# Two transformer blocks: the attentions' arithmetic moved from POOL to DVE and ACT, masks applied on DVE, and attention pieces written between projections

## The chip, the cores and the metric

The kernel runs on one core of one Trainium2 chip. The metric is the device time of one execution in microseconds (us), the median of three runs. The engines are TensorE (PE), VectorE (DVE), ScalarE (ACT), GpSimd (POOL) and SyncE (SP); each works through its own list of instructions in order, and semaphores tie the lists together.

## The reference

Input are 256 tokens of width 1024 and, in block 2, 16 meta tokens ahead of them.

```python
# block 1
h = x + mixer_block(rmsnorm(x), ...)      # sliding-window sink attention + retention, each gated, summed, @ w_out
h = h + squared_relu_mlp(rmsnorm(h), ...)
h = rmsnorm(h)
# block 2, on 16 meta tokens + 256 tokens
qa, ka, va, qb, kb, vb, g = split(rms_norm(h) @ w_in)
qa, ka, qb, kb = rope(qa), rope(ka), rope(qb), rope(kb)
# windowed: 16 query heads on 4 key heads; a key within +-128 positions, every meta key, and a sink logit
p = softmax(concat([where(mask, qa @ ka / 8, -1e30), s_meta, s_sink]))[:, :-1]
o_swa = p @ va
# differential: 8 heads, two softmaxes over all keys each
a = softmax(q1 @ k1 / 8) - lam * softmax(q2 @ k2 / 8)
o_diff = rms_norm(a @ vb) * 0.8
g_swa, g_diff = split(sigmoid(g + b_gate))
merged = g_swa * (o_swa @ w_branch_swa) + g_diff * (o_diff @ w_branch_diff)
h = h + rms_norm(merged @ w_out)
h = h + rms_norm((silu(gate) * up) @ w_ffn_out)
```

## The kernel before

**Weights.** All matrices are cut into 272 units of 128 x 1024 fp32 values (512 KB), in the order of use. SP loads a unit (`raw`), ACT casts it to the rounded part `hi` (L301, two halves of 128x512), DVE forms the rest `lo = raw - hi` (L303), and PE multiplies in three passes (hi·hi, hi·lo, lo·hi), so a unit costs 24 matmuls: of 256 columns where it gives 128 output features for the tokens (`mm_a`, L457), of 272 with the meta tokens, of 512 where the weights are the moving operand (`mm_b`, L469, and `mm_group`, L479). Activations are split alike (`split`: ACT casts, DVE subtracts, L329 and L330).

**Attention.** `rope_T` copies a projection from PSUM (`t`, ACT), has a copy with swapped halves made by DMAs that ACT issues (`sw`, L508 and L509), multiplies by cosines on DVE and by sines on POOL (L511), and adds on POOL (L514). `stack_q` and `stack_k` lay a head's hi and lo parts on the two halves of the partitions (`qe`, `qo`; `ks`, `kl`), with ACT, DVE and POOL. `scores` makes a head's 128 x n scores in PSUM, whose masked part is added by a matmul of an identity with a bf16 mask (`masksb`, L550): 24 of these in block 1, 32 in block 2. `sink_softmax` copies the sink logit beside them, takes the row minimum (the scores are negated), then exponential with its sum, reciprocal, and scaling (L561, L555, L565, L567, L568). `sink_attention`, here a piece, does four heads of one half of the queries; its transposed probabilities (`pt`) are split and multiplied with values (`o_ps`, L587), and the two halves of the result are added (`ol`, `of`).

**Block 1** (`block1`): values, gates, keys and queries of the retention (`vr`, `gr`, `kr`, `qr`), its heads (`ro`, `ry`, `yt_ps`), then the attention on four pieces with the table `rope_a`, which SP loads between two units.

**Block 2** (`block2`): values, `ka`, then for each of four query projections two pieces (eight in all); keys and queries of four pairs of differential heads (`at`, `atm`, `od`, `y`, `ot`), each pair followed by one projection for the first gate; then, in a phase `b3` of its own, the products `bs` of `os_t`, and per group the second gate and the product `bd` of `od_t`, which make `m2t`, the input of the output projection `op`.

**What sets the order.** The code is written in one sequence per engine, but a scheduler of the tile framework reorders each engine's list ahead of time by its own durations, within the dependences and within the numbers of buffers (`BUFS`; PSUM by `BANKS`: two banks each for `acc`, `tp` and `s`, one each for `pv` and `x`). Units are taken strictly in the order of the stream.

Of the kernel before, what the change touches and what calls it, by code (L numbers as in the profile page):

```python
# [37 lines left out]
VB1 = 2  # L38
# [33 lines left out]
def pack_weights(w_in, w_att_up, w_ret_up, w_out, w_ff1, w_ff2, w_in2, w_bs, w_bd, w_out2, w_fi, w_fo):  # L72
# [46 lines left out]
    in_a(w_in2, o_ka)
    for c in range(4):  # L120
        in_a(w_in2, o_qa + 256 * c)
        if c == VB1:
            in_a(w_in2, o_vb + 512)
            in_a(w_in2, o_vb + 768)
    for p in range(4):
        in_a(w_in2, o_kb + 256 * p)
        in_a(w_in2, o_qb + 256 * p)
        in_a(w_in2, o_g + 256 * p)
# [40 lines left out]
def make_consts():  # L169
# [54 lines left out]
class Body:  # L224
# [138 lines left out]
    def consts2(self):  # L363
        nc, cp, io = self.nc, self.cp, self.io
        cc = _CC
        mk = self.wp.tile([P, UC], F32, tag="raw", bufs=4, name="mk")[:, 0:3 * P]
        a, n = cc["masks"]
        nc.sync.dma_start(out=mk, in_=io["consts"][:, a:a + n])
        self.identb = cp.tile([P, P], BF16, name="identb")
        self.masks = cp.tile([P, 3 * P], BF16, name="masksb")  # L370
        nc.gpsimd.tensor_copy(self.identb, self.ident)
        nc.gpsimd.tensor_copy(self.masks, mk)
# [762 lines left out]
```

## Time and profile before

| | us |
|---|---|
| median of three runs (lowest, highest) | 917.32 (916.97, 918.11) |
| the profiled execution: time, span from first to last instruction | 916.5, 914.6 |
| PE busy | 887.4 (97%) |
| DVE, ACT, POOL busy | 628.5, 516.1, 176.7 |
| mean granted clock of TensorE | 0.996 of full speed |

Busy time is the sum of an engine's instructions; the issue of DMAs isn't in it. A time in the rows below is in us from the span's start, a mean in ns. A matmul's row gives when it began; the difference of two beginnings is its step.

### The profile page before, as it was taken

The page shows a single profiled execution, that of the slowest core. Times are in us where ns is not written, and L with a number is a line of the kernel's source. Part 1 is how long each engine was busy: PE and PEld are TensorE (multiplying, and loading weights), DVE is VectorE, ACT ScalarE, POOL GpSimd, SP SyncE. Part 2 cuts the span into 40 slices and gives each one's busy share as a digit, 9 for nine tenths or more (in the row PEclk, how much of TensorE's full clock was granted, in tenths as well). Part 3 has the DMA queues.
Part 4 walks back from the last instruction along what each step waited for, and adds up shares of the span by engine and source line. Part 5 has one row for each costly group of instructions (what it writes and reads, how often), then busy time and mean ns, then how long its engine had stood idle before and what let it go on. Part 6 is the DMA issues. An engine that isn't in the chain of part 4 may idle for free. (4 is left out here: it accounts for less than half of the span.)

```text
span 914.6 us, 16482 instructions
## 1 busy us (share of the span) xinstructions
PE 887.4 (97%) x6188; PEld 814.2 (89%) x6188; DVE 628.5 (69%) x1201; ACT 516.1 (56%) x1128; POOL 176.7 (19%) x181
## 2 busy tenths in 40 slices
PE   5999899999999999999999999999999999999997
PEld 3899889998899999987989878899999799999996
DVE  5466889667755555575689999988567675655654
ACT  4554357554655544565657778876455554544442
POOL 3013460101000011101273434551011100000000
PEclk9999999999999999999999999999999999999999
DMA  7675544468565665562664343433466656555641
GB/s 267 226 232 174 153 150 139 124 223 276 186 213 188 195 189 185 187 227 95 202 200 134 111 126 119 137 107 116 138 182 219 222 200 197 187 199 185 187 161 46
DMA packets 48126, 160.18 MB, mean 175 GB/s; under 512 B 6432, under 2 KB 8224, under 8 KB 48048
## 3 DMA queue, kind: packets, MB, share of 16 engines
q1 hardware_dynamic: 43376, 153.95, 52.1%
q10 hardware_dynamic: 4672, 5.20, 2.0%
q8 instruction: 48, 0.79, 0.3%
q14 instruction: 30, 0.25, 0.1%
HBM read 151.83 MB, written 2.10 MB: 168 GB/s over the span
## 5 line engine op out<-in xcount | busy, mean ns | idle before, releaser
L303 DVE TENSOR_TENSOR lo<-raw,hi 128x512 fp32r<-128x512 f32 x536 | 378.9, 749 | 188.5 <-ACT hi L301 185.3
L301 ACT CAST hi<-raw 128x512 fp32r<-128x512 f32 x532 | 301.8, 618 | 238.7 <-issue 81.8
L469 PE MATMUL op<-hi,hid 128*128 128x512 f32 x416 | 128.9, 390 | 0.0
L457 PE MATMUL fi_ps<-xf2t,hi 128*128 128x256 f32 x640 | 114.4, 281 | 0.0
L457 PEld LDWEIGHTS fi_ps<-xf2t,hi 128*128 128x128 f32 x640 | 99.1, 188 | 0.9
L457 PE MATMUL fi_ps<-xf2t,lo 128*128 128x256 f32 x320 | 90.1, 281 | 0.0
L469 PEld LDWEIGHTS op<-hi,hid 128*128 128x128 f32 x416 | 76.3, 188 | 14.6
L469 PE MATMUL op<-lo,hid 128*128 128x512 f32 x208 | 81.1, 392 | 0.0
L457 PE MATMUL f_ps<-xf1t,hi 128*128 128x256 f32 x448 | 80.5, 281 | 0.0
L457 PEld LDWEIGHTS f_ps<-xf1t,hi 128*128 128x128 f32 x448 | 69.9, 189 | 1.2
L457 PE MATMUL f_ps<-xf1t,lo 128*128 128x256 f32 x224 | 63.0, 281 | 0.0
L457 PEld LDWEIGHTS fi_ps<-xf2t,lo 128*128 128x128 f32 x320 | 60.6, 189 | 0.0
L457 PE MATMUL q_ps<-x2t,hi 128*128 128x256 f32 x256 | 50.3, 287 | 0.0
L457 PE MATMUL gate_ps<-x2t,hi 128*128 128x256 f32 x256 | 48.7, 285 | 0.0
L457 PE MATMUL gate_ps<-x1t,hi 128*128 128x256 f32 x256 | 48.5, 285 | 0.0
L418 POOL TENSOR_SCALAR e<-ss 128x1 f32<-128x1 f32 (+1 forms) x11 | 4.1, 372 | 221.1 <-ACT py L1031 192.2
L469 PEld LDWEIGHTS op<-lo,hid 128*128 128x128 f32 x208 | 39.0, 188 | 8.6
L798 POOL TENSOR_TENSOR sq<-relu 128x512 f32<-128x512 f32 x14 | 15.8, 1130 | 149.7 <-ACT relu L795 149.7
L457 PEld LDWEIGHTS f_ps<-xf1t,lo 128*128 128x128 f32 x224 | 42.4, 189 | 0.1
L457 PEld LDWEIGHTS q_ps<-x2t,hi 128*128 128x128 f32 x256 | 40.4, 189 | 0.8 <-issue 0.5
L457 PEld LDWEIGHTS gate_ps<-x2t,hi 128*128 128x128 f32 x256 | 39.9, 189 | 0.6 <-issue 0.5
L457 PEld LDWEIGHTS gate_ps<-x1t,hi 128*128 128x128 f32 x256 | 39.8, 189 | 0.2
(297 smaller groups left out, 2021.3 us busy)
## 6 DMA issues: line engine op xcount, KB each, us to landing
raw<-in_wstream_dram SPq DMA_DIRECT2D x272, 512.0 KB, 3.7
sw<-t ACTq DMA_DIRECT2D x40, 64.0 KB, 3.7
x<-in_x_dram SPq DMA_DIRECT2D x3, 512.0 KB, 6.5
sw<-t ACTq DMA_DIRECT2D x40, 34.0 KB, 2.2
sw<-t ACTq DMA_DIRECT2D x8, 128.0 KB, 3.5
g_pre<-in_gains_dram SPq DMA_DIRECT2D x2, 512.0 KB, 6.2
x<-hf SPq DMA_DIRECT2D x2, 512.0 KB, 2.7
x<-x SPq DMA_DIRECT2D x2, 512.0 KB, 6.2
```

The costliest lines, as they stand in the source:

```text
L301: nc.scalar.copy(hi[:, c:c + PIECE], raw[:, c:c + PIECE])
L303: nc.vector.tensor_sub(lo[:, c:c + PIECE], raw[:, c:c + PIECE], hi[:, c:c + PIECE].bitcast(F32))
L418: nc.gpsimd.tensor_scalar(out=e[:np_], in0=ss[:np_, 0:1], scalar1=1.0 / D, scalar2=EPS, op0=ALU.mult, op1=ALU.add)
L457: nc.tensor.matmul(out, wv[a][:, k, j * P:(j + 1) * P], XT[:, b, k, n0:n1], start=(i == 0), stop=(i == last))
L469: nc.tensor.matmul(out, XT[:, b, k0 + k, t0:t1], wv[a][:, k, c0:c0 + cn], start=(start and i == 0), stop=(stop and i == last))
L798: nc.gpsimd.tensor_tensor(out=q, in0=r, in1=r, op=ALU.mult)
```

## The change

The masks leave PE: a table of fp32 masks for the two halves of the queries stays in SBUF, and one DVE operation per head adds it, takes the minimum with the sink and writes the masked scores to `pn`. ACT scales by 1/den in place. Rope and the subtractions of `stack_q` are on DVE. `stack_k` splits once and places the parts by four DMAs. These DMAs, and in block 2 the swaps of `rope_T`, are issued by POOL. In block 2 the pieces, the differential heads, the projections, gates and products are written in turn, the phase `b3` is gone, and the stream of units follows. Buffers are dealt anew.

```diff
-        nc.gpsimd.tensor_tensor(out=sw, in0=sw, in1=S, op=ALU.mult)
+        nc.vector.tensor_mul(sw, sw, S)
-        nc.gpsimd.tensor_tensor(out=out, in0=t1, in1=sw, op=ALU.add)
+        nc.vector.tensor_add(out, t1, sw)
@@ stack_q (qo alike)
-        nc.gpsimd.tensor_tensor(out=qe[64:128], in0=qf[0:64], in1=qe[0:64].bitcast(F32), op=ALU.subtract)
+        nc.vector.tensor_sub(qe[64:128], qf[0:64], qe[0:64].bitcast(F32))
@@ stack_k
+        u = self.t([P, 2, n], "ku", F32R)
+        nc.scalar.copy(u[:, 0], kf)
+        nc.vector.tensor_sub(u[:, 1], kf, u[:, 0].bitcast(F32))
...
+            ks = self.t([P, 2, n], "ks", F32R)
+            for b in range(2):
+                nc.gpsimd.dma_start(out=ks[64 * b:64 * b + 64].bitcast(F32), in_=u[64 * e:64 * e + 64].bitcast(F32))
@@ scores
-        for i, (mi, c0) in enumerate(mask or ()):
-            nc.tensor.matmul(out[:, c0:c0 + P], self.identb, self.masks[:, mi * P:(mi + 1) * P],
-                             start=False, stop=(i == len(mask) - 1))
@@ sink_softmax
-        nc.vector.tensor_copy(s[:, n:n + 1], nsink)
-        nm = self.row_min(s)
+        nc.vector.tensor_tensor_reduce(out=p[:, :n], in0=s, in1=mask, scale=1.0, scalar=nsink, op0=ALU.add,
+                                       op1=ALU.min, accum_out=nm)
...
-        nc.vector.tensor_scalar(out=out, in0=p[:, :n], scalar1=rc, scalar2=None, op0=ALU.mult)
+        nc.scalar.activation(out=p[:, :n], in_=p[:, :n], func=AF.Copy, scale=rc)
@@ sink_attention
-        nc.scalar.copy(ol, o[64:128])
...
+            nc.scalar.copy(of[r], o[64:128, e:4:2])
+            nc.vector.tensor_add(of[r], o[0:64, e:4:2], of[r])
@@ block2
+        band(0, 0)
+        for i, b in v_T(4, "vb_ps"):
+            nc.scalar.copy(vall[i][:, 512:1024], b.rearrange("p m d -> p (m d)"))
+        band(0, 1)
+        q[2] = queries()
+        band(1, 0)
+        first_gate(0)
+        band(1, 1)
+        q[3] = queries()
+        band(2, 0)
+        first_gate(1)
+        band(2, 1)
+        kb = keys()
+        band(3, 0)
+        qb = queries()
+        first_gate(2)
+        band(3, 1)
+        first_gate(3)
...
+            self.diff_attention(qb, kb[0:2], vb, OD, 0, 2 * pr)
+            if pr < 3:
+                nk, nq = keys(), queries()
+            else:
+                first_product(3)
+                second_gate(2)
+            self.diff_attention(qb, kb[2:4], vb, OD, 1, 2 * pr + 1)
+            if pr < 3:
+                kb, qb = nk, nq
+                first_product(pr)
+                if pr < 2:
+                    second_gate(pr)
+            else:
+                second_gate(3)
```

On PE, within a piece of windowed attention of block 2, the scores `s` stand in the list of before like this (`vb_ps` is a projection).

```order
L547 MATMUL s<-ks,qe 128x272
L548 MATMUL s<-kl,qe 128x272
L550 LDWEIGHTS identb
L550 MATMUL s<-masksb,identb 128x128
L457 MATMUL vb_ps<-x2t,hi_5868 128x272
L457 MATMUL vb_ps<-x2t,lo_5869 128x272
L547 MATMUL s<-ks,qo 128x272
L548 MATMUL s<-kl,qo 128x272
L550 LDWEIGHTS identb
L550 MATMUL s<-masksb,identb 128x128
```

The masks' loads of the identity and matmuls are gone from every score of the change; here is such a place (`gate_ps` is a projection, `o_ps` a product with the values, `vT_ps` transposes of other values).

```order
L551 MATMUL s<-ks,qe 128x272
L552 MATMUL s<-ks,qe 128x272
L462 MATMUL gate_ps<-x2t,hi_5796 128x256
L961 MATMUL vT_ps<-ident,vt 128x128 x4
L551 MATMUL s<-ks,qo 128x272
L552 MATMUL s<-ks,qo 128x272
L462 MATMUL gate_ps<-x2t,hi_5796 128x256
L462 MATMUL gate_ps<-x2t,lo_5797 128x256
L590 MATMUL o_ps<-pt,va 128x512
```

A score is now its two products, and among the scores stand a gate's projection and the transposes of the values, in another order of the program. At the last piece of windowed attention PE's list of before has projections (`q_ps`) between scores and products `o_ps`:

```order
L547 MATMUL s<-ks,qe 128x272
L548 MATMUL s<-kl,qe 128x272
L457 MATMUL q_ps<-x2t,hi_7186 128x256
L457 MATMUL q_ps<-x2t,lo_7187 128x256
L457 MATMUL q_ps<-x2t,hi_7186 128x256 x2
L587 MATMUL o_ps<-pt,va 128x512
L457 MATMUL q_ps<-x2t,lo_7187 128x256
L457 MATMUL q_ps<-x2t,hi_7186 128x256 x2
L457 MATMUL q_ps<-x2t,lo_7187 128x256
L457 MATMUL q_ps<-x2t,hi_7186 128x256 x2
L457 MATMUL q_ps<-x2t,lo_7187 128x256
L457 MATMUL q_ps<-x2t,hi_7186 128x256 x2
```

In the change the last piece and the first differential head come together, and of projections only the first matmuls of `bs_ps` are among them:

```order
L590 MATMUL o_ps<-pt,va 128x512 x4
L551 MATMUL s<-ks,qe 128x272
L552 MATMUL s<-ks,qe 128x272
L462 MATMUL bs_ps<-os_t,hi_6763 128x256
L590 MATMUL o_ps<-pt,va 128x512
L462 MATMUL bs_ps<-os_t,hi_6763 128x256
L462 MATMUL bs_ps<-os_t,lo_6764 128x256
L462 MATMUL bs_ps<-os_t,hi_6763 128x256 x2
L462 MATMUL bs_ps<-os_t,lo_6764 128x256
L551 MATMUL s<-ks,qo 128x272
L552 MATMUL s<-ks,qo 128x272
L590 MATMUL o_ps<-pt,va 128x512
```

These six are the only matmuls of a projection among the 10 scores, 24 transposes and 13 products of that place, which is 38 rows long; the projections moved ahead of it and behind it. The third place is the last differential head on PE. Before, the last `od` is followed by 38 matmuls of a gate until the head's result is transposed (`ot_ps`):

```order
L977 MATMUL od_ps<-vb,at 128x128
L978 MATMUL od_ps<-vm,atm 128x128
L976 MATMUL od_ps<-vb,at 128x128
L977 MATMUL od_ps<-vb,at 128x128
L978 MATMUL od_ps<-vm,atm 128x128
L457 MATMUL gate_ps<-x2t,hi_8126 128x256
L457 MATMUL gate_ps<-x2t,lo_8127 128x256
L457 MATMUL gate_ps<-x2t,hi_8126 128x256 x2
L457 MATMUL gate_ps<-x2t,lo_8127 128x256
L457 MATMUL gate_ps<-x2t,hi_8126 128x256 x2
```

In the change the second gates stand earlier, and six matmuls of `bd_ps` are between:

```order
L643 MATMUL od_ps<-vb,at 128x128
L644 MATMUL od_ps<-vm,atm 128x128
L642 MATMUL od_ps<-vb,at 128x128
L643 MATMUL od_ps<-vb,at 128x128
L644 MATMUL od_ps<-vm,atm 128x128
L462 MATMUL bd_ps<-od_t,hi_8171 128x256
L462 MATMUL bd_ps<-od_t,hi_8239 128x256
L462 MATMUL bd_ps<-od_t,hi_8171 128x256
L462 MATMUL bd_ps<-od_t,lo_8172 128x256
L462 MATMUL bd_ps<-od_t,hi_8239 128x256
L462 MATMUL bd_ps<-od_t,lo_8240 128x256
L658 MATMUL ot_ps<-ident,y 128x128 x2
```

The rest of `bd_ps` needs the result that `ot_ps` transposes, so nothing else stands there.

## Rows read from the trace of the kernel before

**Rows 1.** The page's busy line: busy time in us, share of the span, instructions of each engine.

```profile
PE 887.4 (97%) x6188; PEld 814.2 (89%) x6188; DVE 628.5 (69%) x1201; ACT 516.1 (56%) x1128; POOL 176.7 (19%) x181
```

**Rows 2.** The table of stretches, block 2's attention: the stretch in us, its length, busy time (and instructions) of PE, PE's weight loads, DVE, ACT and POOL, the granted clock, the DMA engines' busy share, GB/s.

```profile
463.00:585.00 122.00, 117.14 (x868) 105.23 (x867) 116.42 (x265) 94.40 (x232) 63.31 (x51) 1.00 0.43 131
585.00:698.00 113.00, 112.26 (x895) 107.05 (x895) 83.06 (x166) 70.19 (x189) 25.24 (x25) 1.00 0.45 141
```

**Rows 3.** The list of waits, PE's: what waited for what, us in total, times, longest.

```profile
PE ro L692 <- DVE at L688: 2.3, 1, 2.3
PE yt_ps L707 <- DVE ry L702: 1.7, 2, 1.1
PE o_ps L587 <- DVE of L593: 1.6, 2, 1.3
```

**Rows 4.** The chain of waits within 745 to 770 us, two steady pieces of the second MLP: start, us, what, matmuls.

```profile
751.39 11.36 PE fi_ps L457 x96
762.75 5.48 PE op L469 x24
```

**Rows 5.** PE's timeline at a masked score of block 2 (above the dots) and at one without a mask: start, us, operation, count.

```profile
521.01 0.29 PE L548 MATMUL s<-kl,qe 128*128 128x272 f32 x1
521.14 0.23 PE L550 MATMUL s<-masksb,identb 128*128 128x128 bf16 x1
521.18 0.37 PE L457 MATMUL k_ps<-x2t,lo 128*128 128x272 f32 x1
521.39 0.27 PE L583 MATMUL pt_ps<-ident,pn 128*16 128x128 f32 x1
...
550.93 0.29 PE L548 MATMUL s<-kl,qe 128*128 128x272 f32 x1
551.06 0.29 PE L457 MATMUL k_ps<-x2t,lo 128*128 128x272 f32 x1
551.18 0.29 PE L457 MATMUL k_ps<-x2t,hi 128*128 128x272 f32 x1
```

**Rows 6.** PE's timeline at two transposes of a differential head.

```profile
646.25 0.27 PE L964 MATMUL at_ps<-ident,a 128*128 128x128 f32 x1
646.36 0.27 PE L969 MATMUL atm_ps<-ident,a 128*16 128x128 f32 x1
```

**Rows 7.** PE's timeline at the two ends of block 2's attention stretch.

```profile
412.84 0.40 PE L479 MATMUL vb_ps<-hi,x2t 128*16 128x512 f32 x1
...
697.92 0.62 PE L469 MATMUL op<-hi,m2t 128*128 128x512 f32 x2
```

**Rows 8.** DVE's groups of like instructions from 437 to 660 us: line, operation, shapes and count, busy us and mean ns of one, idle time before them and what ended it.

```profile
L303 DVE TENSOR_TENSOR lo<-raw,hi 128x512 fp32r<-128x512 f32 x100 | 82.0, 852 | 9.5 <-ACT hi L301 9.4
L568 DVE TENSOR_SCALAR pn<-p,rc 128x272 f32<-128x272 f32 x32 | 14.9, 495 | 0.2
L555 DVE TENSOR_REDUCE mn<-s 128x1 f32<-128x273 f32 x32 | 13.1, 428 | 0.1
L539 DVE TENSOR_TENSOR kl<-t,ks 64x272 fp32r<-64x272 f32 x20 | 11.3, 564 | 4.4 <-ACT ks L537 4.1
L561 DVE COPY s<-nsink 128x1 f32<-128x1 f32 x32 | 4.2, 147 | 0.1
```

**Rows 9.** ACT's groups from 437 to 660 us, with the same columns.

```profile
L565 ACT ACTIVATE p<-s,mn 128x273 f32<-128x273 f32 x32 | 15.5, 490 | 11.4 <-DVE mn L555 9.6 <-PE q_ps L457 1.7
L565 ACT ACTIVATION_READ_ACCUMULATOR p<-s,mn 128x1 f32 x32 | 6.3, 198 | 0.0
L537 ACT CAST ks<-t 64x272 fp32r<-64x272 f32 x20 | 8.3, 416 | 5.0 <-POOL t L514 4.6 <-PE s L547 0.2
L590 ACT COPY ol<-o_ps 64x512 f32<-64x512 f32 x8 | 4.7, 584 | 1.1 <-ACT t L504 0.6 <-PE pt_ps L583 0.3
L504 ACT COPY t<-k_ps 128x272 f32<-128x272 f32 x10 | 3.8, 381 | 2.2 <-PE k_ps L457 2.0 <-issue 0.2
```

**Rows 10.** DMA issues: on the page, the 34 KB swaps (count, KB each, median us from issue to landing); from the view of line L509, the issuing instructions from 437 to 660 us (duration in ns: lowest, median, highest).

```profile
sw<-t ACTq DMA_DIRECT2D x40, 34.0 KB, 2.2
...
L509 ACTq DMA_DIRECT2D sw<-t x36: 514/601/1235, 442.9 to 606.3; - x36
```

**Rows 11.** POOL's groups from 437 to 660 us, columns as in group 8.

```profile
L511 POOL TENSOR_TENSOR sw<-sw,rope_b 128x512 f32<-128x512 f32 x8 | 13.6, 1703 | 28.7 <-DMA sw<-t 20.4 <-DVE lo L303 8.2
```

**Rows 12.** DVE's group of `lo` from 740 to 900 us, in the second MLP.

```profile
L303 DVE TENSOR_TENSOR lo<-raw,hi 128x512 fp32r<-128x512 f32 x114 | 73.7, 688 | 62.3 <-ACT hi L301 62.2
```

**Rows 13.** Block 1: DVE's timeline at the first use of `rope_a`, PE's at the product behind it (the wait in brackets), the table of stretches there (columns as in group 2), and DVE's timeline at a later `ry`.

```profile
103.65 0.42 DVE L510 TENSOR_TENSOR t<-t,rope_a 128x256 f32<-128x256 f32 x1 [2.49 <-DMA rope_a<-in_consts_dram]
...
105.06 0.81 PE L692 MATMUL ro<-vr,at 128*128 128x256 f32 x2 [2.32 <-DVE at L688]
...
106.00:108.00 2.00, 2.00 (x7) 1.65 (x7) 2.00 (x3) 0.56 (x2) 1.41 (x3) 0.50 0.00 0
...
125.52 0.54 DVE L702 TENSOR_SCALAR ry<-ro,mv,rq 128x256 f32<-128x256 f32 x1 [1.67 <-POOL rq L401]
```

**Rows 14.** The groups of a differential head's end from 437 to 660 us, on ACT, POOL and DVE.

```profile
L982 ACT ACTIVATE y<-od_ps 128x128 f32<-128x128 f32 x16 | 4.3, 279 | 3.4 <-PE od_ps L978 3.4
...
L986 POOL TENSOR_TENSOR rq<-ms,nhalf 128x2 f32<-128x2 f32 x8 | 5.8, 726 | 36.1 <-DVE ms L984 36.1
...
L988 DVE SCALAR_TENSOR_TENSOR y<-od_ps,rq,rows 128x128 f32<-128x128 f32 x16 | 4.9, 346 | 4.3 <-POOL rq L986 4.3
```

More of the change, by code (lines that the diff above doesn't have):

```diff
@@ L37 @@
 SKIP3, SPARE3 = 4, ["DE", "A"]
-VB1 = 2
+ROOM = 48
 PIECE = 512
@@ L117, in pack_weights @@
     in_b(w_in2, o_vb)
+    in_a(w_in2, o_ka)
     in_a(w_in2, o_va)
[L119 to L128, printed above, removed]
+    in_a(w_in2, o_qa)
+    in_a(w_in2, o_qa + 256)
+    in_a(w_in2, o_vb + 512)
+    in_a(w_in2, o_vb + 768)
+    in_a(w_in2, o_qa + 512)
+    in_a(w_in2, o_g)
+    in_a(w_in2, o_qa + 768)
+    in_a(w_in2, o_g + 256)
+    in_a(w_in2, o_kb)
+    in_a(w_in2, o_qb)
+    in_a(w_in2, o_g + 512)
+    in_a(w_in2, o_g + 768)
+    for p in range(3):
+        in_a(w_in2, o_kb + 256 * (p + 1))
+        in_a(w_in2, o_qb + 256 * (p + 1))
+        in_a(w_bs, 256 * p)
+        if p < 2:
+            in_a(w_in2, o_g + 1024 + 256 * p)
+    in_a(w_bs, 768)
+    in_a(w_in2, o_g + 1024 + 512)
+    in_a(w_in2, o_g + 1024 + 768)
     for g in range(4):
-        in_a(w_bs, 256 * g)
-    for g in range(4):
-        in_a(w_in2, o_g + 1024 + 256 * g)
         in_a(w_bd, 256 * g)
@@ L183, in make_consts @@
     j = np.arange(P)[None, :]
-    add("masks", np.concatenate([np.where(j <= i, 0.0, MASKED), np.where(j >= i, 0.0, MASKED),
-                                 np.where(j > i, 0.0, MASKED)], axis=1))
+    le, ge, gt = (np.where(c, 0.0, MASKED) for c in (j <= i, j >= i, j > i))
+    z = np.zeros((P, P))
+    add("masks", np.concatenate([gt, le, z, le, z[:, :NMETA], ge, z, z[:, :NMETA]], axis=1))
     f = _freqs(500000.0, 16)
@@ L365, in consts2 @@
         cc = _CC
[L366 to L372, printed above, removed]
+        mk = self.load("masks", [P, 2 * P + 2 * NKEY])
+        self.mask1 = [mk[:, P:2 * P], mk[:, 0:2 * P]]
+        self.mask2 = [mk[:, 2 * P:2 * P + NKEY], mk[:, 2 * P + NKEY:]]
         self.vec = cp.tile([P, 48], F32, name="vec")
@@ L488, in group_b, with rope_T @@
             yield b[:z - a]
-    def rope_T(self, ps, m, n, tab, half, out=None, scale=1.0):
+    def rope_T(self, ps, m, n, tab, half, out=None, scale=1.0, dma=None):
         nc = self.nc
+        dma = dma or nc.scalar
         tn = tab.shape[-1] // 2
@@ L886, in v_T @@
             vt = []
-            for _ in range(m):
+            for j in range(m):
                 b = self.acc([P, NKEY], name)
                 self.mm_a(b, self.next_unit(), XT, 0, NKEY)
-                f = self.t([P, NKEY], "vt")
-                nc.scalar.copy(f, b)
-                vt.append(f)
+                if j % 2 == 0:
+                    f = self.t([P, 2, NKEY], "vt", tag="ks")
+                nc.scalar.copy(f[:, j % 2], b)
+                vt.append(f[:, j % 2])
             for i, (a, z) in enumerate(toks):
@@ L1012, in block2 @@
+            nc.vector.tensor_add(g, g, MS[:, 2 * gq:2 * gq + 2, :])
+            self.split(MT[:, 0, 2 * gq:2 * gq + 2, 0:NTOK], MT[:, 1, 2 * gq:2 * gq + 2, 0:NTOK], g, 0.5)
         es.close()
```

226 lines of the change are left out of this document (104 added, 122 removed).

## The prediction, made before the changed kernel ran

> **What bounds the kernel now.** I read the busy line first: TensorE (PE) is busy for 887.4 of 914.6 us [rows 1]. It is the engine to shorten, and other engines matter only where PE waits for them or where they do. The table of stretches comes next [rows 2]. From 463 to 585 us, where the eight pieces of windowed attention and the first differential heads lie, DVE is busy for 116.42 of 122 us, ACT for 94.40, POOL for 63.31, and PE stands idle for 122 − 117.14 = 4.9 us. From 585 to 698 us PE is idle for 0.7 us only.
>
> The list of PE's waits shows how little is visible as a wait [rows 3]: 2.3 us for `ro` and 1.7 us for `yt_ps` in block 1, 1.6 us for `o_ps` in the pieces of attention. A PE that is called busy may still be late, so I compare steps with what a steady stretch gives: 96 matmuls of 256 columns in 11.36 us, 0.118 each, and 24 of 512 columns in 5.48 us, 0.228 each [rows 4]; a 272-column one steps by 0.125 to 0.13 us (550.93, 551.06, 551.18) [rows 5]; a transpose by 0.11 (646.25 to 646.36) [rows 6]. The attention stretch of block 2, from the first `vb_ps` at 412.84 to the first `op` on `m2t` at 697.92 us [rows 7], has 1152 matmuls of 256 columns (136 us), 512 of 272 (65), 104 of 512 (24), 32 masks (4, below), and some 340 transposes and small products (42 us by their own steps): 271 of 285.1 us. So about **14 us** of waits and late starts lie there, of which some 5.6 us show as idle. That is the most that any order of block 2 can give back.
>
> **The change, part by part.**
>
> *Masks.* A masked score steps from `kl` at 521.01 over the mask to a projection at 521.18 that runs until 521.39: 0.38 us. Without a mask the same three instants are 550.93, 551.06 and 551.18: 0.25 us [rows 5]. The difference is 0.125 us, times 56 masks = **7.0 us** (24 in block 1, 3.0; 32 in block 2, 4.0). PE's list is otherwise the same set of instructions, so this comes off unless a wait takes its place. What DVE pays: it loses copy 0.147 and minimum 0.428 per head [rows 8]; the fused operation is not in the trace. Its lower bound is a minimum over as many elements, 0.43; its upper one the scaling's 0.495 with a small row for the accumulator (0.147), 0.64, or with an ACT-like reading of the accumulator (0.198 [rows 9]) 0.69. I take 0.59. So DVE pays 32 × 0.59 = 18.9 in block 2 for 17.3 before: nothing, with bounds of −3.5 and +5 us of DVE.
>
> *Scaling by 1/den* goes from DVE (0.495 x32, 14.9 us) [rows 8] to ACT; bounds there are a 272-column copy, 0.381, and the exponential without its accumulator, 0.490 [rows 9]; I take 0.43, 13.8 us of ACT.
>
> *Keys.* `stack_k` loses four half casts (0.416 x2 per tile on ACT) [rows 9], DVE's `kl` (0.564 x20) [rows 8] and POOL's. It gains one cast (about 0.4 us) and one subtraction (0.44) per call, 10 calls, and four DMAs from POOL. The swap DMAs land 2.2 us (34 KB) after their issue [rows 10]; the stacks are of like size, so a key is later by about 2 us plus POOL's issues. Only the first keys (`ka`) have little work to hide it; the diff keys are written a whole head ahead.
>
> *Rope and queries.* POOL's multiply and add (1.703 us for 128x512) [rows 11] and its two query subtractions go to DVE: at the clean 0.688 us for 128x512 [rows 12] this is 8 × 2 × 0.69 + 10 × 2 × 0.44 = 19.8 us for rope and 16 × 0.69 = 11.0 us for queries. DVE's own `lo` takes 0.852 us here and 0.688 in the MLP, where POOL is idle [rows 8, 12]; if that excess is POOL's doing, the 100 `lo` give back 0.164 each, 16 us, and DVE's other operations with two inputs perhaps 6: 22 us. Sum for DVE: −43.5 (scaling, minimum, copy, `kl`) + 19 + 20 + 11 + 4 = +10 and −22: about −12 of 212 us in this stretch. ACT: −16.7 (key casts) − 4.7 (`ol`) + 13.8 + 6.4 (`of`) + 4.2 = +3 us, and it is rid of 72 DMA issues of 0.5 to 0.6 us [rows 10], nearly 40 us of its queue.
>
> On that excess the Trainium skill, "SBUF — State Buffer", section "SBUF: two separate sides", says that a DVE instruction with two SBUF inputs and a GpSimd instruction that reads SBUF exclude each other for a whole instruction. The trace agrees (0.852 against 0.688 us); by the rule all of the excess comes back, and the sum stays.
>
> *POOL's queue.* 112 DMA issues in block 2 (72 swaps, 40 key stacks) and 4 in block 1 take the place of about 110 us of arithmetic. POOL has issued none before; the nearest row is ACT's 0.5 to 0.6 us, so 65 us; at twice that 130 us over about 250 us, still not full, but each later by 0.6. Behind them on POOL stand only `rq` of each diff head and the sink copies.
>
> *Block 1.* DVE waits 2.49 us for the `rope_a` table at 103.65 with `at` behind it, PE then 2.32 us for `ro`, and the granted clock is 0.50 from 106 to 108 [rows 13]: the lower level, at which 105.5 to 108.9 costs another 1.7 us. The table now stands one raw load earlier on SP, and its earlier readers end on DVE. `yt_ps` waits for DVE's `ry`, which waits for `rq` on POOL (1.67 us at 125.52) [rows 13], where it stands behind a rope product; that work leaves POOL. 2.3 + 1.7 + 1.7 = 5.7 us; bounds are 0 (other waits take over) and 6; I take **−4.5**.
>
> *Block 2's order.* Between two pieces there are now two to four units. A unit of 24 × 0.118 is 2.8 us, a gap thus 6 to 11 us, while a piece costs DVE about four times 0.59 + 0.15 and three splits (0.68 each by `lo`'s clean size), two sums and a split of the output: about 6.5 us, and the units' own `lo` on top. These parts balance, DVE is 12 us lighter and ACT's queue 40, so I let them give back 11 of the 14 us. Two places are worse. (1) As the order rows of the last piece show, it and the first head come with six matmuls of a projection among them: about 10 us of PE work, in which ACT has ten exponentials (0.490 + 0.198), six splits (0.584 by `ol`), five scalings (0.43) and two more copies: 13.5 us, and DVE about as much, in chains. PE waits 4 to 10, I take **6.5**. (2) At the end, in the last order rows, six matmuls (0.7 us) stand between the last `od` and `ot`. The chain there is two squares on ACT (0.279 each [rows 14], and about 0.2 for the accumulator as in [rows 9]), `rq` 0.726, two `y` of 0.346 [rows 14] and a small one: 2.5 us or more, for two heads, and before it `at` and `atm` (0.58 and 0.36 by sizes of [rows 9]). Before the change 38 gate matmuls (4.5 us) hid it. I take **6** (4.5 to 7). The first keys' later arrival costs 1.5. Block 2's waits change by −11 + 6.5 + 6 + 1.5 = **+3 us**, from 14 to 17.
>
> **Sum:** −7.0 − 4.5 + 3 = −8.5 us. The profiled execution's own time is 916.5, 0.8 below the median; I set the sum against the median, 917.3, giving **909**.
>
> **Rivals.** (B) *DVE was the brake.* DVE's 95% in 463 to 585 is the bound, and its relief together with ACT's 40 us of issues lets the dense stretch overlap: block 2's friction falls from 14 to about 9 us, the sum is −7 − 5.7 − 5 = −17.7: about 899. For it: no other engine is near 95% there [rows 2]. Against: PE's idle time was 4.9 us only.
>
> (C) *The chains without filler decide.* Where POOL took a share of the arithmetic before, four dependent steps (fused minimum, exponential, reciprocal, scaling) now alternate between DVE and ACT, both in-order queues that also serve `hi` and `lo`. A head costs 0.59 + 0.69 + 0.15 + 0.43 = 1.9 us of latency, and in the two places nothing covers it; with 0.64 + 0.49 and the `lo` of late units between, PE waits 13 and 9 us there instead of 6.5 and 6, and 4 more in the gaps. It ends slower once block 2's waits pass 14 + 7 + 4.5 = 25.5 us; with 14 − 11 + 13 + 9 + 4 + 1.5 = 30.5 us they make 922 (917 to 926). For it: 13.5 us of ACT work against 10 of PE; against: in the gaps DVE and ACT have less to do than before, and a wait in one place leaves `hi` and `lo` ready for the next.
>
> (D) *POOL's issues are slow.* At 2 us each 112 issues are 224 us over some 250; swaps queue behind stacks and each projection's queries come late. That is 925 or more. The same page and section of the Trainium skill hold a rule for it: POOL makes the descriptors itself and cannot while DVE runs an operation of the copy, cast or tensor-scalar kind in its two-port mode; 0.62 us became 3.1 us. No run here shows it; by its figures, estimated, 112 × 3.1 = 347 us would overfill the stretch. Against it stands the order of DVE: its copies and scalings in block 2 (L561, L568) are what this change removes.
>
> (E) *Nothing comes of it*: PE's 7 us of masks go into waits on the fused minimum, block 1 stays: 916 to 919.
>
> **How the numbers follow.** Chances: forecast 0.48 (904 to 914), B 0.19, E 0.11, C 0.16, D 0.06. A difference below about 0.2%, 1.8 us, can't be told from none here. Faster than 915.5: forecast and B, 0.67; same 0.11; slower C and D, 0.22. The range **897 to 921** holds the forecast, E, most of B (0.15) and the lower part of C (0.07), 0.81 in all; it leaves out D and the tails of B and C. The likeliest alone is 904 to 914.
>
> **What would show it.** Right: no mask rows on PE; `lo` near 0.69 us in 437 to 660; `ro` and `yt_ps` gone from PE's waits and no stretch at the lower clock near 106; PE waits in the last piece and before the last `ot`, each 4 to 10 us. Wrong: PE waits spread over the gaps (C); POOL's issue rows of over 1 us with swaps landing late (D); `lo` still at 0.85, so that POOL wasn't its cause; a clock that falls after a long wait, which would double what the wait costs.

## The result and the profile after

The changed kernel takes 928.31 us (median of four runs, 926.62 to 929.22) against 917.14 us for the kernel before beside it: 1.0118 times as long, with an interval of 1.0101 to 1.0136. The forecast was 909. The profiled execution, the longest of the four, has a span of 927.4 us, 12.9 more than before.

Where the time went is read from instructions that both traces have, by the moment at which PE begins them (us from the span's start, worked out from the two timelines):

| PE begins | before | after | shift |
|---|---|---|---|
| first product of block 1's out projection (`op` on `m1t`) | 209.23 | 199.03 | −10.20 |
| first `vb_ps` of block 2 | 412.84 | 402.64 | −10.20 |
| first `op` on `m2t` | 697.92 | 701.84 | +3.91 |
| first `fi_ps` of the last MLP | 721.15 | 727.06 | +5.91 |
| last `fi_ps` | 897.24 | 904.25 | +7.01 |
| end of the span | 914.55 | 927.42 | +12.87 |

So block 1 gains 10.2 us, block 2's attention loses 14.1, the way from the out projection into the MLP loses 3.1 (two waits, on either side of the first `fi_ps`), and 5.9 us are lost behind the last matmul. The busy line, which answers to [rows 1], shows none of that: PE is even 0.9 us less busy.

```profile
PE 886.5 (96%) x6132; PEld 816.1 (88%) x6132; DVE 609.5 (66%) x1216; ACT 523.0 (56%) x1155; POOL 117.1 (13%) x211
```

The table of stretches does (columns as in [rows 2]), first of the kernel before:

```profile
65.00:150.00 85.00, 80.01 (x631) 77.08 (x630) 67.79 (x148) 43.36 (x97) 32.82 (x35) 0.98 0.49 155
463.00:560.00 97.00, 92.71 (x685) 82.89 (x684) 92.97 (x220) 72.58 (x180) 48.63 (x39) 1.00 0.44 132
560.00:590.00 30.00, 29.43 (x218) 26.46 (x217) 28.39 (x55) 26.00 (x62) 16.02 (x14) 1.00 0.41 126
670.00:690.00 20.00, 20.00 (x172) 20.00 (x171) 13.15 (x18) 10.35 (x21) 3.22 (x2) 1.00 0.64 186
```

Then of the changed kernel:

```profile
65.00:150.00 85.00, 85.00 (x693) 83.80 (x693) 69.85 (x170) 51.73 (x121) 12.61 (x22) 1.00 0.55 173
...
412.00:463.00 51.00, 42.11 (x292) 40.19 (x291) 25.41 (x45) 22.78 (x46) 12.06 (x24) 0.90 0.56 177
463.00:560.00 97.00, 96.91 (x758) 91.44 (x757) 81.53 (x212) 84.14 (x212) 22.85 (x49) 1.00 0.53 163
560.00:590.00 30.00, 25.33 (x148) 20.24 (x147) 23.49 (x57) 21.27 (x59) 3.37 (x7) 0.89 0.20 63
590.00:670.00 80.00, 80.00 (x641) 76.95 (x640) 58.78 (x132) 48.65 (x131) 23.57 (x44) 1.00 0.61 183
670.00:690.00 20.00, 17.08 (x104) 14.96 (x103) 7.99 (x20) 7.31 (x23) 1.38 (x2) 0.83 0.12 41
```

In 463 to 560 us, in the gaps between the pieces, PE is idle for 0.1 us, where it was idle for 4.3 before; that gain came, though not by the new order alone (experiment 7). Three places lose: 8.9 us idle ahead of the pieces, 4.7 us at the last piece and the first head (the dense place), 2.9 us at the last heads (the tail), and the mean clock is below 1 in each. The list of PE's waits names them:

```profile
PE vT_ps L961 <- ACT vt L956: 8.9, 1, 8.9
...
PE xt_ps L441 <- DVE xn L1086: 3.0, 2, 1.9
PE ot_ps L658 <- DVE y L654: 2.1, 2, 1.3
PE s L551 <- ACT p L610: 2.0, 4, 0.9
PE pt_ps L586 <- DVE rl L616: 1.3, 1, 1.3
PE bs_ps L462 <- DVE os_t L339: 1.0, 1, 1.0
```

`ro` and `yt_ps` of [rows 3] are gone. The largest wait is new. ACT's timeline there, then POOL's and PE's:

```profile
434.56 0.41 ACT L538 CAST ku<-t 128x272 fp32r<-128x272 f32 x1
441.73 0.42 ACT L538 CAST ku<-t 128x272 fp32r<-128x272 f32 x1 [6.76 <-DMA ks<-ku]
442.06 0.67 ACT L956 COPY vt<-va_ps 128x272 f32<-128x272 f32 x2
...
436.10 2.06 POOL L544 DMA_DIRECT2D ks<-ku  x4 [4.55 <-DVE ku L539]
...
442.49 0.60 PE L961 MATMUL vT_ps<-ident,vt 128*16 128x128 f32 x2 [8.89 <-ACT vt L956]
```

`ku` has one buffer. ACT's second cast into it waits 6.76 us until POOL's four DMAs have read the first, and the copies `vt`, ready for long, stand behind it in ACT's list; PE, whose next work is the transposes of `vt`, waits 8.89 us. The clock, told by the stretches below, then stays at its lower level after the wait:

```profile
436.00:442.00 6.00, 0.00 (x0) 0.00 (x0) 0.88 (x2) 0.27 (x1) 2.06 (x4) 0.66 0.62 193
442.00:448.00 6.00, 5.51 (x26) 5.45 (x27) 0.87 (x3) 1.35 (x5) 2.04 (x4) 0.50 0.37 96
```

At the end, the view of the program's last line gives POOL's closing DRAIN (duration in ns: lowest, median, highest), first of the kernel before, then of the change:

```profile
L1128 POOLq DRAIN  x3: 34/82/659, 909.5 to 914.3; - x3
```

```profile
L1164 POOLq DRAIN  x3: 34/98/10149, 916.5 to 927.2; - x3
```

It begins at 916.5 us, when POOL's list is at its end, and lasts 10.15 us where it was 0.66; the other engines are done at 921.5 and wait for it.

The prices, in the groups of the change, answer to [rows 8], [rows 9] and [rows 10]: `lo`, the fused mask and minimum with its reading of the accumulator, the scaling on ACT and POOL's issues (437 to 670 us, POOL's from 400 to 720).

```profile
L312 DVE TENSOR_TENSOR lo<-raw,hi 128x512 fp32r<-128x512 f32 x104 | 67.6, 685 | 12.4 <-ACT hi L310 11.6
L564 DVE CUSTOM_DVE_ANT_0 pn<-s,masks,nsink 128x272 f32<-128x272 f32 x32 | 14.8, 493 | 1.8 <-PE s L552 0.7 <-PE pt_ps L586 0.5 <-PE q_ps L462 0.4
L564 DVE DVE_READ_ACCUMULATOR2_ANT mn<- 128x1 f32 x32 | 2.6, 81 | 0.0
L570 ACT ACTIVATE pn<-pn,rc 128x272 f32<-128x272 f32 x32 | 15.5, 515 | 0.0
L544 POOL DMA_DIRECT2D ks<-ku x40 | 20.6, 524 | 31.8 <-DVE ku L539 23.2 <-DVE p L624 4.1 <-PE s L552 3.0
L514 POOL DMA_DIRECT2D sw<-t x36 | 18.1, 503 | 103.5 <-ACT t L510 62.5 <-ACT t L512 39.6 <-DVE mn L564 1.4
```

The page gives the landings of POOL's DMAs, 4.1 us for the stacks and 3.6 for the small swaps:

```profile
ks<-ku POOLq DMA_DIRECT2D x40, 136.0 KB, 4.1
...
sw<-t POOLq DMA_DIRECT2D x40, 34.0 KB, 3.6
```

### The profile page after: what moved, and what is told of

The parts are those of the page before. It is cut to its first block, busy times and chain, and to the rows that moved or that the text cites. A ratio compares the mean times of both kernels' runs of the same rounds, so it can differ in the third digit from the quotient of the medians.

```text
span 927.4 us, 16417 instructions
## 1 busy us (share of the span) xinstructions
PE 886.5 (96%) x6132; PEld 816.1 (88%) x6132; DVE 609.5 (66%) x1216; ACT 523.0 (56%) x1155; POOL 117.1 (13%) x211
## 4 chain that ended last, share of the span: by engine, by line
PE 90%; DMA 4%; DVE 2%; ACT 2%; issue 1%; POOL 1%; SPq 0%; DVEq 0%; POOLq 0%; ACTq 0%
PE op L474 18%; PE fi_ps L462 12%; PE gate_ps L462 10%; PE f_ps L462 9%; PE q_ps L462 5%; PE k_ps L462 3%; PE bd_ps L462 2%; PE vr_ps L484 2%; PE ru_ps L462 2%; PE gr_ps L462 2%; DMA raw<-in_wstream_dram 2%; PE bs_ps L462 2%; PE vb_ps L484 2%; PE o_ps L590 2%; PE pt_ps L586 1%; PE vb_ps L462 1%
## 5 line engine op out<-in xcount | busy, mean ns | idle before, releaser
L312 DVE TENSOR_TENSOR lo<-raw,hi 128x512 fp32r<-128x512 f32 x536 | 351.0, 695 | 185.1 <-ACT hi L310 179.5
L462 PE MATMUL q_ps<-x2t,lo 128*128 128x256 f32 x128 | 37.1, 290 | 0.0
L462 PE MATMUL gate_ps<-x2t,lo 128*128 128x256 f32 x128 | 36.6, 286 | 0.0
```

Source lines behind the costliest of these rows:

```text
L312: nc.vector.tensor_sub(lo[:, c:c + PIECE], raw[:, c:c + PIECE], hi[:, c:c + PIECE].bitcast(F32))
L462: nc.tensor.matmul(out, wv[a][:, k, j * P:(j + 1) * P], XT[:, b, k, n0:n1], start=(i == 0), stop=(i == last))
```

## The experiments

The scheduler writes new lists for every edit. PE's list of matmuls is the same only in experiment 1 and the kernel before, in 7 and 10, and in 12 and 13; in experiment 5 it is that of before from the first MLP on. Elsewhere a difference in time belongs to the edit together with the lists that came with it.

**1. One DMA of POOL in the kernel before.**

```diff
-        nc.sync.dma_start(out=self.vec[:, 0:40], in_=io["vec"])
+        nc.gpsimd.dma_start(out=self.vec[:, 0:40], in_=io["vec"])
```

> The kernel before, with one small load of block 1 (the gate biases, 20 KB) issued by POOL; SP issued it before. In the trace of the change POOL's closing drain runs from 916.49 to 926.64 us, 10.15 us, where it took 0.60 before, and the last engine instruction of the change ends 5.8 us later behind the last output DMA than before. Theory 'any POOL DMA': the long drain belongs to a program that has issued even one DMA from POOL; the end moves by 5.9 us, 917.1 -> 923.0. Rival 'amount': the drain works off what 116 DMAs left behind; one DMA long past costs 0.05 us, 917.1 +- 0.5.

Measured: 917.33 us, 1.0008 times before (0.9992 to 1.0024). The drain is 0.755 us:

```profile
L1128 POOLq DRAIN  x3: 40/89/755, 909.9 to 914.8; - x3
```

So "any POOL DMA" fell; the drain depends on how much POOL has issued.

**2. All DMAs issued by ACT.**

```diff
-                nc.gpsimd.dma_start(out=ks[64 * b:64 * b + 64].bitcast(F32), in_=u[64 * e:64 * e + 64].bitcast(F32))
+                nc.scalar.dma_start(out=ks[64 * b:64 * b + 64].bitcast(F32), in_=u[64 * e:64 * e + 64].bitcast(F32))
...
-                kf = self.rope_T(b, 1, NKEY, rope_b, 32, dma=nc.gpsimd)
+                kf = self.rope_T(b, 1, NKEY, rope_b, 32)
```

(and the same for the queries.)

> The changed kernel, with all of POOL's DMAs (72 swaps, 44 key stacks) issued by ACT. Theory 'drain': the closing drain is short again and 5.9 us go; ACT pays 116 issues of 0.5 to 0.6 us, some 64 us of its queue, of which what falls into the stretch from 463 to 585 us (half of it, ACT is at 101 of 122 us there) shows as PE waits of some 5 us more: 928.3 - 5.9 + 5 = 927, within 922 to 932. Rival 'POOL issues delay the DMAs': landings fall from 3.6 and 4.3 us (swaps) and 4.1 us (stacks) to the 2.2 and 3.7 us of before, the key wait of 8.9 us and its lower clock shrink by 3 us or more: below 922.

Measured: 931.63 us, 1.016 times before (1.0145 to 1.0175). The drain is short again (0.67 us), but the wait for `vt` grew from 8.9 to 14.1 us, and the first `op` on `m2t` came 9.1 us later than in the change. This is the first theory, at the upper end of its range: the drain goes, and ACT's queue costs more than that gives. "POOL issues delay the DMAs" fell: issued by ACT, the small swaps and the stacks both land after 3.8 us, where POOL's took 3.6 and 4.1.

**3. More buffers for `ku`.**

```diff
-        u = self.t([P, 2, n], "ku", F32R)
+        u = self.t([P, 2, n], "ku", F32R, tag="ks")
```

(with `ks=9`, and no buffer of its own for `ku`.)

> The changed kernel; the split key 'ku', which has one buffer, takes its buffers from the nine of 'ks' instead. In the trace of the change ACT's second cast of ku waits 6.76 us until the four DMAs of the first have read it; the copy 'vt' stands behind it on ACT, PE waits 8.9 us for the transposes of vt, and the clock is at its lower level from 438 to 447.6 us. Theory 'one buffer': wait and clock go, 8.9 + 2.6 = 11.5 us: 928.3 -> 916.8. Rival 'first keys are late anyway': the DMAs' landing (4.1 us behind POOL's four issues of 0.5) still ends the first scores' wait, so that PE waits at the first scores instead: only 3 to 6 us, 922 to 925.

Measured: 919.06 us, 1.0019 times before (1.0005 to 1.0033): 9.2 us of the change's loss, between what the theory and the rival expected. PE still waits 4.0 us for `vt`, now because the second cast waits 1.87 us for its rope product with `vt` behind it.

**4. Masks alone, in the kernel before.**

```diff
+        nm = self.sm(1, "mn")
+        nc.vector.tensor_tensor_reduce(out=p[:, :n], in0=s, in1=mask, scale=1.0, scalar=nsink, op0=ALU.add,
+                                       op1=ALU.min, accum_out=nm)
...
+        nc.scalar.activation(out=p[:, :n], in_=p[:, :n], func=AF.Copy, scale=rc)
```

(and no mask matmuls; for space, the buffers `p` of the differential heads are 5, not 6.)

> The kernel before with the masks alone changed: the fused sum and minimum on DVE, the scaling by 1/den on ACT, the sink column by POOL, no mask matmuls; rope, stacks, DMAs and order as before. Theory of the prediction: 56 matmuls of 0.125 us go and DVE and ACT pay nothing that shows: 917.1 - 7.0 = 910. Rival 'masks were cheap': PE stood late in the pieces anyway, so block 1's 24 and block 2's 32 masks lay in its waits: 915 to 917. Rival 'chain': the fused operation (0.493 + 0.081 us in the change) and the scaling on ACT (0.515) lengthen ACT's queue in 463 to 585 us by 32 x 0.5 = 16 us: 918 to 922.

Measured: 924.51 us, 1.0076 times before (1.0061 to 1.0092). Block 1 gains 3.9 us up to the first `vb_ps`, as 24 masks of 0.125 and a little more; block 2's attention loses 10.3. Its table of stretches:

```profile
463.00:585.00 122.00, 113.30 (x817) 104.40 (x816) 96.74 (x220) 100.06 (x248) 53.74 (x51) 0.96 0.43 133
```

Two of PE's waits in it:

```profile
PE s L546 <- DVE mn L559: 4.5, 4, 2.5
PE ot_ps L990 <- DVE y L986: 2.5, 2, 1.6
```

DVE fell from 116.42 to 96.74 us [rows 2] and PE became idler all the same. The rival "chain" is nearest, and it was given too small a size. A second cause is not separated from it. The fused operation writes `pn`, which is free again only when PE has transposed it; this version has two buffers of `pn`, the change three, and DVE waits there:

```profile
DVE pn L559 <- PE pt_ps L581: 5.8, 3, 3.0
```

So this loss cannot be carried over to the masks of the change as it stands.

**5. Block 1 of the change, block 2 of before.**

> Block 1 of the change (rope and stack_q on DVE, fused masks, stacks by four DMAs from POOL, its buffers), with block 2 of the kernel before, masks on PE included. Theory: block 1's gain is whole and its own, the first op on m1t came 10.2 us earlier in the change: 917.5 - 10.2 = 907, with a short closing drain, since only 4 DMAs are POOL's. Rival 'drain from SBUF copies': four DMAs between SBUF addresses are enough for the long drain (the one load that kept it short came from DRAM): 913. Rival: block 2 takes it back through another start of the stream of units: 910 to 917.

(The edit calls copies of the changed functions from `block1` alone.) Measured: 913.56 us, 0.9964 (0.9952 to 0.9977). The gain is 8.8 us at the first `op` on `m1t`, 7.1 at the first `vb_ps` and 4.6 at the first `op` on `m2t`: the first MLP and block 2, whose code did not change, gave part of it back. PE's list is that of before in both, and in block 2's attention so are DVE's and POOL's, so other orders hardly explain it; why it was given back stays open. The drain of four DMAs is 1.0 us, and the rival on the drain fell.

```profile
L1231 POOLq DRAIN  x3: 34/102/1004, 906.5 to 911.6; - x3
```

**6. Buffers and ACT's issues together.** The edits of 2 and 3.

> The changed kernel with both: ku in the buffers of ks, and all DMAs of POOL issued by ACT. Measured so far: the buffers alone 919.1, ACT's issues alone 931.6, where the wait for vt grew from 8.9 to 14.1 us. Theory: with the buffers the key wait no longer hangs on the issue, the closing drain (10.15 us in both runs with POOL's DMAs, 0.67 without) is short: 919.1 - 5.9 + 3 of ACT's queue = 916. Rival 'ACT's queue is the bound of the pieces': 116 issues of 0.5 to 0.6 us bring 10 us or more of PE waits between 460 and 590: 923 or more.

Measured: 931.82 us, 1.0146 (1.0118 to 1.0175): the rival. Compared with 3, 5.9 us of drain are saved and the first `op` on `m2t` comes 21 us later. 116 more issues of 0.5 to 0.6 us cost more on ACT than the drain on POOL does.

**7. The arithmetic of the change in the order of before.** Edit 3, and block 2's code and stream in the sequence of the kernel before, with `va` ahead of `ka` and the phase `b3` again at the end.

> The arithmetic of the change (masks fused, rope and stacks off POOL, POOL's DMAs, ku in the buffers of ks) in the order of before in block 2: va ahead of ka, two pieces per query projection without units between, gates behind each pair of heads, the phase b3 at the end. Compared with the same arithmetic in the new order, 919.1. Theory 'arithmetic': the masks alone, in the order of before, lost 10.3 us in block 2; ACT and DVE bound the pieces in either order, so this one is slower than 919.1: 922 to 928, of which 5.9 is the closing drain. Rival 'order': the new order makes the dense place and the uncovered tail (some 9 and 3 us with the buffers); without it 905 to 912.

Measured: 911.95 us, 0.9943 (0.9925 to 0.9961), 7.1 us below experiment 3. So "arithmetic" fell: with POOL's issues it is no loss. The 7.1 us are the whole order's, with `va` ahead of `ka` in it (experiment 12 gives that alone). In 463 to 585 us PE is idle for 0.35 us only, so the gaps close without units written between the pieces:

```profile
463.00:585.00 122.00, 121.65 (x930) 113.14 (x928) 108.26 (x265) 103.08 (x254) 39.46 (x83) 1.00 0.57 174
```

The dense place and the tail are in this version too, the first of them mostly behind that stretch: the scheduler's list has no matmul of a projection from 581.2 to 595.2 us, and three ahead of the last `ot_ps`. PE is idle for 2.0 and 2.2 us around them, at a mean clock of 0.83 and 0.89:

```profile
575.00:605.00 30.00, 28.00 (x169) 23.97 (x168) 24.29 (x64) 21.57 (x67) 8.73 (x17) 0.83 0.38 113
640.00:655.00 15.00, 12.80 (x85) 11.64 (x84) 5.65 (x14) 5.86 (x18) 1.38 (x2) 0.89 0.29 101
```

**8. The swaps alone, issued by POOL, in the kernel before.**

```diff
-            nc.scalar.dma_start(out=sw[p:p + half], in_=raw[p + half:p + 2 * half])
+            nc.gpsimd.dma_start(out=sw[p:p + half], in_=raw[p + half:p + 2 * half])
```

> The kernel before with the 80 swap DMAs of rope issued by POOL, where ACT issued them; all arithmetic as before. Theory on the drain: it is long (10.15 us) once there are many DMAs of POOL: the end moves by 5.9 us. On the issues: ACT is rid of 40 us of its queue, PE's waits in the pieces are small there (4.9 us), so at most 3 us come back, while POOL's rope products stand behind the issues and each swap lands 0.6 to 1.4 us later: 917.5 + 5.9 + 0 to 3 = 922 to 926. Rival: ACT's queue held the pieces back, 917.5 + 5.9 - 8 = 915.

Measured: 912.67 us, 0.9949 (0.9932 to 0.9966). The last `fi_ps` begins 9.1 us earlier; 5.6 of them are won in block 1 and 3.3 in block 2's attention. A drain of 8.19 us takes 3.9 us back:

```profile
L1128 POOLq DRAIN  x3: 34/102/8189, 900.4 to 909.1; - x3
```

Its table of stretches:

```profile
463.00:585.00 122.00, 120.68 (x910) 109.45 (x909) 115.00 (x275) 96.00 (x241) 82.63 (x98) 1.00 0.45 134
```

The stretch differs from [rows 2] in PE (117.14 to 120.68) while ACT's busy time and DVE's stay within 2 us. What was taken from ACT, 92 issues (the expectation has 80; it left out 12 in block 1), was in no busy time. The rival had the direction; of the 8 us that it gave to the pieces, block 2's attention shows 3.3. In block 1 the wait for `ro` and the low clock at 106 us are gone, with the load of `rope_a` and rope's arithmetic as before. But some 1270 of PE's 6188 matmuls stand in another place of the list than before, so how much is ACT's queue and how much the new order isn't shown. An issue takes POOL 0.503 us in the median, and the 34 KB swaps land after 2.8 us (2.2 when ACT issued them [rows 10]).

**9. Both: masks and swaps by POOL.** The edits of 4 and 8.

> The kernel before with two edits: the fused masks (alone 924.5, slower by 6.6) and the swap DMAs issued by POOL (alone 912.7, faster by 5). Theory 'ACT's queue': the masks lost because their scaling (32 x 0.515 us) fell on an ACT that is busy for 94 of 122 us from 463 to 585 and issues some 45 DMAs of 0.5 to 0.6 us besides, which no busy time counts; with the issues gone the masks' 7 us of PE come through: 912.7 - 5 = 908, within 905 to 911. Rival 'the chain in DVE and ACT': minimum, exponential, reciprocal, scaling alternate between the engines whoever issues the DMAs; the masks lose what they lost before, 912.7 + 6.6 = 919.

Measured: 916.14 us, 0.9985 (0.9965 to 1.0005), between the two expectations. Without the issues the masks lose 3.5 us (916.1 against 912.7) where they lost 6.6 with them; in block 2's attention alone they lose 2.2 us by the traces where they lost 10.3. So ACT's queue is likely part of the cause, with the lists as a rival, and not all of it; what is left shows as waits of PE for `mn` (2.0) and `ot_ps` (1.9), and one in block 1 (`au_ps`, 2.2). How much of this is the one buffer of `p` less, or the two of `pn`, isn't told apart.

**10. The drain off the end.** Experiment 7, with the last norms' instructions of POOL moved:

```diff
+        def rnorm_dve(ss):
...
+            nc.scalar.activation(out=r, in_=m, func=AF.Sqrt)
+            nc.vector.reciprocal(r, r)
...
-            for c, s in post(t, acc, g_po):
+            for c, s in post(t, acc, g_po, rnorm_dve):
```

> The change's arithmetic in the order of before (912.0, closing drain of POOL 10.15 us), with the last norms' four POOL instructions on DVE and ACT (square root there, reciprocal on DVE). The drain stood behind POOL's last instruction, 6 us ahead of the end. Drains so far: 0.66 us without POOL DMAs, 0.76 with 1, 1.0 with 4, 8.19 with 80, 10.15 with 116: some 0.085 us for each. Theory: the drain works off what was issued and starts as soon as POOL's list is done, now 170 us before the end; it is hidden, 912.0 - 5.9 = 906. Rival: the drain needs the other engines' end first: 912 again.

Measured: 907.09 us, 0.9907 (0.9883 to 0.9931). The drain is as long as ever, but it begins at 717.9 us and nobody waits for it:

```profile
L1147 POOLq DRAIN  x3: 34/98/10151, 717.9 to 908.1; - x3
```

PE's list is that of experiment 7, so no other order of PE's work stands behind the difference. It is the lowest median of the study, 1% below the kernel before; experiment 13 can't be told from it.

**11. A combination.** Block 1 of the change, block 2 of before with its swaps issued by POOL, the last norms off POOL.

> A combination, as a candidate for the fastest: block 1 of the change (alone -7.1 us at the first product of block 2), block 2 of before with its swap DMAs issued by POOL (there -3.3 us between the first vb and the first op on m2t), and the last norms off POOL so that the drain of 76 DMAs is hidden. If the three add: 917.7 - 8 - 3.3 - 0 = 906. If block 2 depends on where the stream of units stands when it begins (block 1's gain alone shrank from 8.8 to 3.3 us by the end): 909 to 912.

Measured: 909.54 us, 0.9934 (0.9909 to 0.9959), the upper case: block 1's 8.9 us are 7.2 at the first `vb_ps`, as in experiment 5. By the span (908.0 us, the drain of 6.88 us hidden) the parts add only nearly.

**12. `va` ahead of `ka`.** Experiment 3, with the two projections and their units exchanged.

> The change with ku in the buffers of ks (919.1; PE still waits 4.0 us for the transposes of vt and 1.3 at the lower clock), and va projected ahead of ka as in the kernel before, so that vt stands ahead of both key casts on ACT. Theory: this wait goes whole, 919.1 - 5 = 914. Rival: the first scores wait instead, since the keys' DMAs now start 5.7 us later: 917 to 919.

Measured: 914.40 us, 0.9972 (0.9955 to 0.999): 4.7 us below experiment 3, and the wait for `vt` is gone from PE's list. The expected 914 came about. Against experiment 7, which has the same arithmetic and the same drain, the new order loses 2.4 us by the medians, with intervals that overlap; in the two traces the first `op` on `m2t` begins at 688.17 and 688.09 us, so no place of block 2 is shown to lose them.

**13. The change with the three mended.** Experiment 12 and the last norms of experiment 10.

> The change with three edits: ku in the buffers of ks (measured 928.3 -> 919.1), va ahead of ka (-> 914.4), and the last norms off POOL, which hid the drain in the other order (912.0 -> 907.1). If these three are the whole of what the prediction left out (its 909.0 against 928.3, 19.3 us), this runs at 914.4 - 5.5 = 909, within 907 to 911, and what is left of the new order's dense place and tail is what the prediction priced. If the order holds more that these waits only covered, it stays above 911.

Measured: 909.14 us, 0.9905 (0.9878 to 0.9933). So the three causes make up the 19.2 us between the forecast, 909.0, and the measured 928.3; other terms that missed cancel (below). Against experiment 10, the other order with the drain hidden, the ratios are 0.9905 and 0.9907: apart from `va` and `ka`, no difference between the two orders is shown. What is left on PE's list are, above all, waits of the dense place and the tail, and `xt_ps` on the way into the MLP:

```profile
PE pt_ps L586 <- DVE pt L339: 2.2, 2, 1.4
PE xt_ps L441 <- DVE xn L1096: 2.0, 2, 1.0
PE s L551 <- ACT p L610: 1.9, 2, 1.2
PE ot_ps L658 <- DVE y L654: 1.3, 1, 1.3
```

## Why the prediction was wrong, step by step

- **The end.** The sum had no term for it. POOL's issues were priced where they stand, 0.5 to 0.6 us each (0.50 measured) and 65 us of its queue; that they leave a closing drain was not among the steps. It cost 5 to 6 us (4.9 by the medians of experiments 7 and 10, 5.3 by those of 12 and 13, in each pair with PE's list unchanged; in the change's trace the span ends 5.9 us later behind the last matmul than before). No row of the trace before could show it, since POOL issued no DMA there.
- **The first keys, "the first keys' later arrival costs 1.5".** This is the step that failed most. It looked at when the key reaches the scores, not at what stands behind the key on ACT. (It also took the stacks to be of like size as the 34 KB swaps; they are 136 KB and land after 4.1 us.) A wait for the four DMAs' reading (one buffer) held ACT's list, `vt` stood in it, and PE waited 8.9 us and then ran at the lower clock until about 448 us. The buffers gave back 9.2 us, `va` ahead of `ka` another 4.7: 13.9 us in place of 1.5. Of these the change's trace shows 11.7 at the place, 8.9 of wait and about half of the 5.7 us that PE then ran at the lower clock; where the rest came off isn't shown. The rule of the prediction's own working, to name what is queued behind an instruction that begins to wait, was applied to POOL and not to ACT.
- **Block 1, −3.0 for masks and −4.5 for waits.** Right in kind and too small: −10.2. `ro`, `yt_ps` and the low clock at 106 us went, and from 65 to 150 us PE's idle time went from 5.0 to 0 us. The masks alone gave 3.8 of it (experiment 4). The reasons given for the rest, the earlier load of `rope_a` and the work that left POOL, weren't tested one by one, and `ro` and the low clock go without them in experiment 8.
- **The gaps, −11.** Near: from 463 to 560 us PE's idle time fell from 4.3 to 0.1 us, and late starts went with it. The working credited the units between the pieces, DVE's relief and ACT's; the units aren't needed, since experiment 7 has the gain in the order of before. Experiment 8 gains without less work on DVE, so ACT's issues are the likelier part, with its new lists as a rival. `lo` at 0.685 us bears out that its excess came with POOL's arithmetic: in the trace before, the 47 of them that ran beside an instruction of POOL took 1.04 us in the mean, 52 others 0.68. But in experiment 8 `lo` stays at 0.850 and the kernel is faster all the same.
- **The masks, −7.0.** The matmuls went. Whether their 4 us in block 2 came off isn't shown: in the order of before the fused masks alone lose there (experiments 4 and 9), but with fewer buffers of `pn` than the change has. The sum let DVE and ACT pay nothing; the scaling on ACT, priced at 0.43 us per head, took 0.515, and was set against casts that left in another part of the change.
- **The dense place, +6.5 (4 to 10), and the tail, +6 (4.5 to 7).** Right in place, and near in size: compared with steady steps the change loses 9.6 us from 560 to 590 and 7.4 us from 670 to 690, the second above its bound of 7, the lower clock after the waits included, which the sum had left out. The reason given, too few matmuls of projections between the chains, fits, but the order in which the code is written isn't what makes it: experiment 7, written in the order of before, loses in both places too, and its list has no such matmul from 581.2 to 595.2 us and three ahead of the last `ot_ps`. It is the scheduler's list; why it comes out so with this arithmetic is open. PE's timeline of the change at the two:

```profile
568.83 0.63 PE L586 MATMUL pt_ps<-ident,pn 128*128 128x128 f32 x4 [1.30 <-DVE rl L616]
572.93 0.38 PE L462 MATMUL bs_ps<-os_t,hi 128*128 128x256 f32 x1 [1.00 <-DVE os_t L339]
...
675.62 0.59 PE L658 MATMUL ot_ps<-ident,y 128*128 128x128 f32 x2 [0.83 <-DVE y L654]
680.34 0.66 PE L658 MATMUL ot_ps<-ident,y 128*128 128x128 f32 x2 [1.31 <-DVE y L654]
```

- **The way into the MLP.** Not in the sum: 3.1 us, PE's wait for `xt_ps`. It is 2 to 2.7 us in the list of experiments 3, 10 and 13 too. DVE waits there for the gain `g_pm`, whose DMA lands 16.8 us behind the first `op` where it was 14.9. What delays it was not tried and stays open.
- **The rivals.** D had the time right, 925 or more, for a reason that fell: POOL's issues take 0.50 us and the 34 KB swaps land after 3.6. C had the two places and, with the chains that nothing covers, their kind; but they cost 9.6 and 7.4 us, not 13 and 9, and the gaps cost nothing, so they didn't decide the time. The rule of the Trainium skill, "SBUF — State Buffer", section "SBUF: two separate sides", by which POOL's DMAs starve beside DVE's copies and scalings in their two-port mode, could be looked at in experiment 8, whose DVE still does both in the pieces: issues of 0.50 us in the median, at most 0.62 for the 12 that ran beside a scaling (L568), and landings after 2.8 us against 2.2, so 0.6 us each and nothing like the 2.5 us that the page's figures differ by. Whether these scalings run in that mode no row shows.

With the three causes mended the kernel runs at 909.1 (experiment 13). That is the forecast, but not proof of each of its terms. In the trace of 13, whose execution is 2 us below the median, block 1 gains 10.1 us where the sum had 7.5, block 2's attention gains 2.6 where it had 2.5 without the first keys, and 3.5 us are lost behind the first `op` on `m2t`, where it had no term. That these errors cancel is luck.

## What to carry to other kernels

When a step becomes a DMA out of a single buffer, look at the list of the engine that next writes this buffer: its wait holds everything behind it, and that may be work that PE needs at once. Count an engine's DMA issues with its busy time before calling another engine the limit; here 92 issues of 0.5 to 0.6 us stood in no busy time of ACT, and without them, in new lists, the last `fi_ps` came 9 us earlier. Moving DMAs to POOL had a price at the program's end, 5 to 6 us here, and none where POOL's list ended early. Where a scheduler rewrites the lists, compare them before a gain is put down to the edit: here two written orders came out with the same two bare places.

## What had not been expected of the hardware

POOL's closing DRAIN grows with what POOL has issued: 0.66 us with no DMA, 0.76 with one, 1.0 with 4, 6.88 with 76, 8.19 with 92 (two runs) and 10.15 us with 116 (the same in every run with these 116). From 76 on that is 0.082 us for each above the 0.66. It takes that long even when it starts more than a hundred microseconds after POOL's last issue (experiment 10: 717.9 against 589.5 us), so it is no wait for transfers under way. When POOL's list ended early, it cost nothing.
